# Block products for the down projection of three middle parts of the second feed-forward, added into x in DRAM

## The chip, the cores and the metric

The kernel runs on one core of a Trainium2 chip. The metric is the device time of one execution in microseconds (us); smaller is better. Three runs of the kernel before gave 1496.33, 1497.17 and 1498.62 us, so its median is 1497.17 us. One more execution was taken with the hardware profiler: it took 1496.28 us, of which the trace spans 1493.9 us, so 2.4 us lie around the span, and it is 0.9 us below the median.

The engines go by short names: PE is the matrix engine (TensorE), DVE is VectorE, ACT is ScalarE, POOL is GpSimd, SP is SyncE, which here only starts transfers. PSUM is the memory in eight banks that PE accumulates in, SBUF the large on-chip memory.

## The reference

One step through a two-layer backbone. Layer 0 has neighbourhood attention, layer 1 a gated linear recurrent unit, and behind each stands a gated feed-forward, with scale, shift and gate from a condition vector:

```
def _swiglu(x, w_gu, w_down):
    gate, up = jnp.split(x @ w_gu, 2, axis=-1)
    return (jax.nn.silu(gate) * up) @ w_down
...
        f_c = _swiglu(_modulate(ctx, norm_g[i, 1], sh2_c, sc2_c), ffn_w_gu[i], ffn_w_down[i])
        f_l = _swiglu(_modulate(lat, norm_g[i, 1], sh2_l, sc2_l), ffn_w_gu[i], ffn_w_down[i])
        ctx = ctx + g2_c[:, None, :] * f_c
        lat = lat + g2_l[:, None, :] * f_l
    y_prompt = _rms_norm(ctx, final_g)
    y_sample = _rms_norm(lat, final_g)
```

There are 128 context and 512 latent tokens, 640 in all; the model width is 1024 (8 tiles of 128) and the hidden width 2816 (22 tiles). The gate vector g2 differs between context and latent tokens. All is float32. The change bears on the down projection `@ w_down` of layer 1 and on the gated addition to the residual x behind it, and in a small way on the end of layer 0's attention.

## The kernel before, in words

**Numbers.** PE takes operands in a rounded 32-bit form (fp32r in the trace). Each operand is split in a high part (a cast) and a low part (the operand minus its high part), and each product is three matmuls: high by high, high by low, low by high. `split` does the two steps: the cast on ACT (L1496) and the subtraction on DVE (L1497). `chunk` (L251) is a plain product: for each of its k tiles of the inner dimension it issues the three matmuls of L252, L253 and L254, each 128 columns of weights by 320 tokens.

**The second feed-forward.** `ffn_halves` (L1220) walks over the 22 hidden tiles in six parts of 3, 3, 4, 4, 4 and 4 (CHN). For each hidden tile it makes gate and up, multiplies silu(gate) by up, splits the product in `hhi` and `hlo`, and when a part is done its rows of the down projection follow. Gate and up of one hidden tile are computed as one 2x2 block product with seven half products in place of eight (the scheme of Strassen and Winograd). Each of the seven is one call of `product` (L1167), three matmuls (L1171, L1172, L1173) for each of four k tiles. Its outputs accumulate in three PSUM banks: `mx` takes A11·B11, then S2·T2, then S3·T3, then A22·T4 on top of one another; `mm` takes A12·B21; `mc` takes S1·T1 and then S4·B22. A running sum that is needed by itself is copied out by ACT (`snap`, L1177) before PE may add the next product to the bank. In a part, `pair_a`, `pair_b` and `pair_c` hold these steps for a hidden tile; the weights' sums S1 to S4 are made by POOL (L1144), and cast and subtracted by ACT and DVE like the rest. `hidden` (L1187) ends a tile: multiply on DVE (L1190), cast on ACT, subtract on DVE, for each half of the tokens (320 each).

**The down projection of parts 1 to 5**, `project_part` (L603): for each of the eight output tiles and each half of the tokens, four k tiles (three in the first two parts) by three matmuls in a bank `mm`; `residual` (L569) then adds the gated sum to x in SBUF on DVE (L574), in pieces of 192, 128 and 320 columns, since the gate changes between context and latent tokens. A part of four tiles has 4·7·4·3 = 336 matmuls for gate and up, and 8·2·4·3 = 192 for the down projection. `project_last` does it for part 6, with the final norm.

**The order.** A scheduler simulates the program when it is built and sets the order of each engine's instructions; at the places in question the code adds a few rules of what issues after what (`issue_after`). On the chip every engine then runs its list in order, and a waiting instruction holds up all behind it. The plain down projection of a part can begin over the hidden tiles that are done, so at a part's end PE has a stock of matmuls that wait for nothing; the scheduler puts them between a bank's last matmul and the next one that has to wait for a copy of it.

**The end of the attention.** In layer 0 the output projection begins while the last heads are computed; the attention's result O is split tile by tile (ohi, olo), with rules for when the splits of the last tiles may issue (L1588).

## Time and profile before

| view | value |
|---|---|
| median of three runs | 1497.17 us |
| the profiled execution | 1496.28 us |
| its span | 1493.9 us |
| PE busy, share of the span | 1467.3 us, 98% |
| DVE busy | 1087.8 us, 73% |
| ACT busy | 730.4 us, 49% |
| POOL busy | 280.7 us, 19% |
| granted PE clock, mean | 0.997 of full speed |

Busy time of an engine is what its instructions took; matmuls are pipelined, so a matmul that lasts 0.31 us is followed by the next after 0.147 us. The views that matter here are the table by stretches of time (busy time of each engine within a stretch, with the number of instructions in brackets), the list of waits of one engine, the timeline (start, duration, engine, line, operation, tile written <- tiles read, and in square brackets the idle time before it with what ended it), the groups of instructions (count | busy us, mean ns of one | idle time before them) and the list of transfers (issuing queue, count, size, median time from issue to landing).

### The profile page before, as it was taken

Reading aid. Unit: us, or ns where it says so; the run is one execution under the profiler, and the core shown is the slowest. Engines: PE = TensorE matmul, PEld = TensorE weight load, DVE = VectorE, ACT = ScalarE, POOL = GpSimd, SP = SyncE. Lnnn points to the kernel's source line nnn. Section 1 sums busy time; section 2 is a strip of 40 time slices with the busy share of each in tenths; the row PEclk is TensorE's granted clock in tenths of the full one; section 3 lists DMA queues with packets and bytes.
Section 4 is the critical chain, followed back from the end, with each engine's and each line's share of the span. In section 5 each row is a group of like instructions: output and inputs, shape, how many; then the busy total and the mean of one; then the engine's idle time right before and its main releaser. Section 6 shows DMA issues by size and latency. Waiting matters only on the chain. (4 is left out here: it accounts for less than half of the span.)

```text
span 1493.9 us, 26401 instructions
## 1 busy us (share of the span) xinstructions
PE 1467.3 (98%) x10369; PEld 1438.2 (96%) x10369; DVE 1087.8 (73%) x2050; ACT 730.4 (49%) x1344; POOL 280.7 (19%) x357
## 2 busy tenths in 40 slices
PE   7999999999999999999999999999999999999997
PEld 4999999899999999999999999999999999999997
DVE  5788887868748779997766479985875566665655
ACT  5666766754334334422344298864634343424244
POOL 0212121100102222221210001112122332232311
PEclk9999999999999999999999999999999999999999
DMA  9554645445429999885863744266242131313111
GB/s 373 176 158 144 187 150 156 125 141 172 142 90 329 320 336 338 308 288 186 290 210 118 250 151 142 85 232 245 84 131 85 57 113 57 113 57 104 67 57 71
DMA packets 86427, 255.39 MB, mean 171 GB/s; under 512 B 9456, under 2 KB 22944, under 8 KB 86176
## 3 DMA queue, kind: packets, MB, share of 16 engines
q1 hardware_dynamic: 59408, 157.06, 32.1%
q0 software_dynamic: 26576, 96.49, 18.7%
q8 instruction: 81, 1.33, 0.3%
q14 instruction: 42, 0.34, 0.1%
q10 hardware_dynamic: 320, 0.16, 0.0%
HBM read 206.22 MB, written 43.53 MB: 167 GB/s over the span
## 5 line engine op out<-in xcount | busy, mean ns | idle before, releaser
L253 PE MATMUL mm<-big,whi 128*128 128x320 f32 (+3 forms) x1010 | 313.9, 311 | 1.9 <-DVE big L1497 1.9
L252 PE MATMUL mm<-big,whi 128*128 128x320 f32 (+3 forms) x1010 | 312.1, 311 | 3.2 <-ACT big L1496 2.1
L254 PE MATMUL mm<-big,wlo 128*128 128x320 f32 (+3 forms) x1010 | 313.7, 311 | 0.2 <-DVE wlo L1497 0.2
L291 DVE SCALAR_TENSOR_TENSOR mprod<-mraw,csb 128x1024 f32<-128x1024 f32 x160 | 195.9, 1224 | 19.2 <-DMA mraw<-in_wm 18.4
L252 PEld LDWEIGHTS mm<-big,whi 128*128 128x128 f32 x1010 | 190.1, 189 | 5.5 <-ACT big L1496 3.0
L253 PEld LDWEIGHTS mm<-big,whi 128*128 128x128 f32 x1010 | 190.9, 189 | 3.7 <-DVE big L1497 2.6
L254 PEld LDWEIGHTS mm<-big,wlo 128*128 128x128 f32 x1010 | 190.8, 189 | 1.5 <-DVE wlo L1497 0.4
L1496 ACT CAST whi<-raw 128x1024 fp32r<-128x1024 f32 (+2 forms) x103 | 105.7, 1026 | 152.0 <-PE mm L253 84.7
L1497 DVE TENSOR_TENSOR wlo<-raw,whi 128x1024 fp32r<-128x1024 f32 (+2 forms) x103 | 127.0, 1233 | 37.7 <-ACT whi L1496 37.3
L253 PE MATMUL mm<-big,whx 128*128 128x320 f32 (+3 forms) x443 | 137.4, 310 | 0.0
L254 PE MATMUL mm<-big,wlx 128*128 128x320 f32 (+3 forms) x443 | 137.1, 310 | 0.0
L252 PE MATMUL mm<-big,whx 128*128 128x320 f32 (+3 forms) x443 | 136.8, 310 | 0.0
L574 DVE SCALAR_TENSOR_TENSOR x<-mm,G,x 128x320 f32<-128x320 f32 (+3 forms) x202 | 81.5, 436 | 55.2 <-PE mm L254 50.1
L287 POOL DMA_DIRECT2D mraw<-in_wm x80 | 43.4, 543 | 313.5 <-DVE mprod L291 213.8
L254 PE MATMUL mx<-big,wlo 128*128 128x320 f32 (+3 forms) x318 | 99.2, 312 | 0.0
L253 PE MATMUL mx<-big,whi 128*128 128x320 f32 (+3 forms) x318 | 99.0, 311 | 0.0
L252 PE MATMUL mx<-big,whi 128*128 128x320 f32 (+3 forms) x318 | 98.7, 311 | 0.0
L253 PEld LDWEIGHTS mm<-big,whx 128*128 128x128 f32 x443 | 83.5, 189 | 0.0
L254 PEld LDWEIGHTS mm<-big,wlx 128*128 128x128 f32 x443 | 83.5, 189 | 0.0
L252 PEld LDWEIGHTS mm<-big,whx 128*128 128x128 f32 x443 | 83.4, 188 | 0.0
L253 PE MATMUL mx<-big,whx 128*128 128x320 f32 (+3 forms) x229 | 71.4, 312 | 0.0
L254 PE MATMUL mx<-big,wlx 128*128 128x320 f32 (+3 forms) x229 | 71.3, 312 | 0.0
(387 smaller groups left out, 3864.7 us busy)
## 6 DMA issues: line engine op xcount, KB each, us to landing
raw<-in_gu SPq DMA_DIRECT2D x84, 512.0 KB, 3.8
mraw<-in_wm POOLq DMA_DIRECT2D x80, 512.0 KB, 4.9
raw<-in_dn SPq DMA_DIRECT2D x24, 512.0 KB, 3.6
raw<-in_wqk SPq DMA_DIRECT2D x16, 512.0 KB, 4.0
sw<-in_wm SPq DMA_DIRECT2D x16, 512.0 KB, 10.2
mraw<-in_wi POOLq DMA_DIRECT2D x16, 512.0 KB, 6.4
kwi<-kwh POOLq DMA_DIRECT2D x16, 512.0 KB, 6.0
kwi<-kwl POOLq DMA_DIRECT2D x16, 512.0 KB, 5.6
```

The source lines that it names most:

```text
L252: nc.tensor.matmul(ps, hi[:, k], xhi[:, k, s], start=(k == 0), stop=False)
L253: nc.tensor.matmul(ps, hi[:, k], xlo[:, k, s], start=False, stop=False)
L254: nc.tensor.matmul(ps, lo[:, k], xhi[:, k, s], start=False, stop=(k == nk - 1))
L287: nc.gpsimd.dma_start(w, self.i["wm"][l * 6 + j - 2, f])
L291: nc.vector.scalar_tensor_tensor(prod, w, 1.0, self.csb[:, s], ALU.mult, ALU.mult, accum_out=out[:, s, f:f + 1])
L574: last = self.nc.vector.scalar_tensor_tensor(xs, ps[:, a - t0:b - t0], G[:, s, f:f + 1], xs, ALU.mult, ALU.add).ins
L1496: high = self.nc.scalar.copy(hi, v).ins
L1497: return high, self.nc.vector.tensor_tensor(lo, v, hi.bitcast(F32), ALU.subtract).ins
```

## The change

Parts 3, 4 and 5 (`BLOCKS = (2, 5)`) get another down projection. It is now a 2x2 block product as well: output tile f and output tile f+4 are the two block rows, the two halves of the tokens the block columns, and even and odd hidden tiles of the part the inner blocks. It takes seven half products of two k tiles, so 7·2·3 = 42 matmuls for a pair of output tiles and 4·42 = 168 for a part.

- `hidden` no longer writes the plain product h for these parts but what the scheme needs: of each pair of hidden tiles B11, T1 = B12 - B11, B21 and B22, and after the fourth also T2 = B22 - T1, T3 = B22 - B12 and T4 = B21 - T2. The last three go to a new tile `hx`.
- There is no room for `hx` beside x. So after part 2 x is stored to DRAM (`xd`, eight transfers of SP), `hx` takes its place in SBUF (the order names it x for that reason), and after part 5 x is loaded again by four transfers of SP.
- In `project_blocks` the weights of a pair of output tiles come by four transfers of 128 KB in place of one of 512 KB; POOL makes four sums of 128x256, ACT casts 768 and 1024 columns, where it cast 1024 for two output tiles, and DVE subtracts as many.
- The sums leave PSUM through `gated`, by ACT (scale by the gate) or by DVE (scale, and add an earlier copy); pieces that reach over the border between context and latent tokens take two instructions, of 192 and 128 columns. The results are added to `xd` in DRAM by accumulating transfers that POOL issues, three for a pair of output tiles.
- Apart from that, at the end of the attention the splits of O for k = 2 and 3 are to issue after the last Exp, and one after the other.

```
-    def project_part(self, w, hi, lo, gk):
+    def project_part(self, w, hi, lo, gk, store):
...
+                if store:
+                    self.nc.sync.dma_start(self.xd[(f + j) * P:(f + j) * P + P], self.x[:, f + j])
...
+        n = 2 * (j % 2) + c
+        if n == 0:
+            one = self.t([P, NTOK], F32, "ssq", 1, self.sb)
+            self.hb = [self.t([P, HT], F32, "sq", 2, self.sb) for _ in range(2)] + [one[:, 0:HT], one[:, HT:]]
+        t1, b12, b21, b22 = self.hb
+        h = self.hb[n]
+        nc.vector.tensor_tensor(h, u, g, ALU.mult)
+        if n == 1:
+            nc.vector.tensor_tensor(t1, b12, t1, ALU.subtract)
+            h = t1
+        self.split(hi, lo, h)
+        if n == 3:
+            for o, u, v in ((t1, b22, t1), (b12, b22, b12), (b21, b21, t1)):
+                nc.vector.tensor_tensor(o, u, v, ALU.subtract)
+            for m, v in enumerate((t1, b12, b21)):
+                self.split(self.hx[:, j // 2, m, 0], self.hx[:, j // 2, m, 1], v)
+
+    def gated(self, o, ps, G, f, t0, v=None):
+        for s, a, b in _pieces(t0, t0 + HT):
+            g, r = G[:, s, f:f + 1], slice(a - t0, b - t0)
+            if v is None:
+                self.nc.scalar.activation(o[:, r], ps[:, r], AF.Copy, scale=g)
+            else:
+                self.nc.vector.scalar_tensor_tensor(o[:, r], ps[:, r], g, v[:, r], ALU.mult, ALU.add)
+        return o
+
+    def project_blocks(self, w, gk, mid):
...
+        for f in range(KH):
+            raw = self.t([P, KT, P], F32, "raw", 3)
+            for a, (g, j) in enumerate(((f, 0), (f, 1), (f + KH, 1), (f + KH, 0))):
+                nc.sync.dma_start(raw[:, 2 * a:2 * a + 2], w[g].rearrange("p (k t) m -> p t k m", t=2)[:, j])
+            s = self.t([P, KT, P], F32, "sum", 2, self.sb)
...
+            for o, u, v, op in ((s1, a21, a22, ALU.add), (s2, s1, a11, ALU.subtract), (s3, a11, a21, ALU.subtract), (s4, a12, s2, ALU.subtract)):
+                nc.gpsimd.tensor_tensor(o, u, v, op)
...
+            def add(g, t0, o):
+                nc.gpsimd.dma_start(self.xd[g * P:g * P + P, t0:t0 + o.shape[1]], o, accum_op=ALU.add)
+
+            def kept(ps, g, t0):
+                return self.gated(self.t([P, HT], F32, "snap", 3, self.sb), ps, G, g, t0)
+
+            b = self.ps("mx")[:, 0:HT]
+            product(b, "A11", "B11", True)
+            m1 = kept(b, f, 0)
+            a = self.pg(False)[:, 0:HT]
+            product(a, "A12", "B21", True)
+            add(f, 0, self.gated(self.t([P, HT], F32, "sq", 2, self.sb), a, G, f, 0, m1))
+            c = self.ps("mc")[:, 0:HT]
+            product(c, "S1", "T1", True)
+            product(b, "S2", "T2", False)
+            u2 = kept(b, f, HT)
+            product(b, "S3", "T3", False)
+            u3 = kept(b, f + KH, HT)
+            o = self.t([P, NTOK], F32, "ssq", 1, self.sb)
+            self.gated(o[:, HT:], c, G, f + KH, HT, u3)
+            product(c, "S4", "B22", False)
+            add(f, HT, self.gated(self.t([P, HT], F32, "yo", 1, self.sb), c, G, f, HT, u2))
+            product(b, "A22", "T4", False)
+            self.gated(o[:, 0:HT], b, G, f + KH, 0)
+            add(f + KH, 0, o)
...
                     for k in range(4):
-                        with tc.issue_after(self.evac if k < 2 else self.low), tc.issue_after(self.cast) if k > 1 else nullcontext():
-                            self.split(ohi[:, k], olo[:, k], O[:, k])
+                        with tc.issue_after(self.evac) if k < 2 else tc.issue_after(self.low1), tc.issue_after(self.exp) if k > 1 else nullcontext(), tc.issue_after(self.cast) if k > 1 else nullcontext():
+                            high, low = self.split(ohi[:, k], olo[:, k], O[:, k])
```

The orders of the two programs show how matmuls and copies now stand. All tile numbers are those of the built programs; `mx_14360` is the same bank use in one row as in the next.

PE before, at the end of part 4, where the product S3·T3 of its last hidden tile (the 14th of 22) ends and A22·T4 adds to the same bank. The rows of L252, L253 and L254 are matmuls of the same part's down projection over its first hidden tiles.

```order
L1173 MATMUL mx_14360<-big_11765,wlx_14404 128x320
L253 MATMUL mm_14583<-big_11765,whi_14579 128x320
L254 MATMUL mm_14583<-big_11764,wlo_14580 128x320
L254 MATMUL mm_14597<-big_11764,wlo_14580 128x320
L252 MATMUL mm_14597<-big_11764,whi_14579 128x320
L253 MATMUL mm_14597<-big_11765,whi_14579 128x320
...
L1171 MATMUL mx_14360<-xt_11353,wuh_14440 128x320
```

PE after the change, the same step of the same hidden tile.

```order
L1174 MATMUL mx_14484<-big_11765,whx_14527 128x320
L1175 MATMUL mx_14484<-big_11765,whx_14527 128x320
L1176 MATMUL mx_14484<-big_11765,wlx_14528 128x320
L1174 MATMUL mx_14484<-xt_11353,wuh_14568 128x320
L1175 MATMUL mx_14484<-xt_11353,wuh_14568 128x320
L1176 MATMUL mx_14484<-xt_11353,wul_14569 128x320
```

Before, nine matmuls of the down projection stood between the end of one product in the bank and the start of the next; after the change the next product stands directly behind.

ACT after the change, at the end of the same part and the first pair of output tiles (the casts to `x_13265` write T2, T3 and T4 to `hx`; L1218 is `gated`).

```order
L1596 CAST big_11764<-ssq_14543 128x320
L1596 CAST x_13265<-sq_14544 128x320
L1596 CAST x_13265<-sq_14545 128x320
L1596 CAST x_13265<-ssq_14543 128x320
L1218 ACTIVATE snap_14744<-mx_14712,G_1498_8333 128x192
L1218 ACTIVATE snap_14744<-mx_14712,G_1498_8333 128x128
L1218 ACTIVATE snap_14753<-mx_14712,G_1498_8333 128x192
L1218 ACTIVATE snap_14753<-mx_14712,G_1498_8333 128x128
```

The three casts for `hx` and four pieces that empty the bank `mx_14712` have come in; on PE the products S2·T2, S3·T3 and A22·T4 of that pair of output tiles stand directly behind one another in this bank.

DVE at the end of a part, after the change (`g` is silu(gate) or its sum, `ssq` and `sq` hold B and T parts, L1210 is `hidden`'s subtractions).

```order
L1185 TENSOR_TENSOR g_14691<-mm_14678,snap_14676 128x320
L1597 TENSOR_TENSOR wlx_14875<-sum_14865,whx_14874 128x1024
L1203 TENSOR_TENSOR ssq_14543<-c_2351_14613,g_14642 128x320
L1210 TENSOR_TENSOR sq_14544<-ssq_14543,sq_14544 128x320
L1210 TENSOR_TENSOR sq_14545<-ssq_14543,sq_14545 128x320
L1597 TENSOR_TENSOR big_11765<-ssq_14543,big_11764 128x320
L1210 TENSOR_TENSOR ssq_14543<-ssq_14543,sq_14544 128x320
L1597 TENSOR_TENSOR x_13265<-sq_14544,x_13265 128x320
L1597 TENSOR_TENSOR x_13265<-sq_14545,x_13265 128x320
L1220 SCALAR_TENSOR_TENSOR sq_14728<-mm_14721,G_1498_8333,snap_14719 128x320
L1597 TENSOR_TENSOR x_13265<-ssq_14543,x_13265 128x320
```

Before, the same place had the multiply of L1190, one subtraction of L1497 and then the additions to x of L574; now three subtractions of L1210 and three of L1597 stand behind the last multiply, ahead of what the next products read. Over the whole program PE's list goes from 9492 to 9420 rows, DVE's from 1817 to 1859 and ACT's from 1203 to 1306.

More of the change, by code (lines that the diff above doesn't have):

```diff
@@ L49 @@
 CHN = (3, 3, 4, 4, 4, 4)
+BLOCKS = (2, 5)
 START = (
@@ L145, in __init__ @@
         self.n, self.ng, self.nu, self.hold, self.late = 0, 0, 0, None, []
-        self.anchor, self.pbufs, self.lastq, self.whole, self.nraw, self.px = None, {}, {}, False, 2, None
+        self.anchor, self.pbufs, self.lastq, self.whole, self.nraw, self.px, self.low = None, {}, {}, False, 2, None, None
     def nm(self, s):
@@ L1189, in hidden @@
         hi, lo = [t[:, j, c * HT:c * HT + HT] for t in (self.hhi, self.hlo)]
-        nc.vector.tensor_tensor(g, u, g, ALU.mult)
-        self.split(hi, lo, g)
+        if self.hx is None:
+            nc.vector.tensor_tensor(g, u, g, ALU.mult)
+            self.split(hi, lo, g)
+            return
+        n = 2 * (j % 2) + c
+        if n == 0:
+            one = self.t([P, NTOK], F32, "ssq", 1, self.sb)
+            self.hb = [self.t([P, HT], F32, "sq", 2, self.sb) for _ in range(2)] + [one[:, 0:HT], one[:, HT:]]
@@ L1223, in ffn_halves @@
         f0 = 0
+        self.hx = None
         for ci, n in enumerate(CHN):
```

48 lines of the change are left out of this document (42 added, 6 removed).

## Prediction

> **What bounds the kernel now.** I read the page's first two parts, then the table by stretches of time for the second feed-forward, then PE's own list of waits there. The page says who is busy:
>
> ```profile
> PE 1467.3 (98%) x10369; PEld 1438.2 (96%) x10369; DVE 1087.8 (73%) x2050; ACT 730.4 (49%) x1344; POOL 280.7 (19%) x357
> PE   7999999999999999999999999999999999999997
> PEclk9999999999999999999999999999999999999999
> ```
>
> PE has work in every slice at full granted clock. The three middle parts are three equal stretches (columns: stretch, its length, then busy us and count of PE, weight loads, DVE, ACT, POOL, and last the clock, the DMA share and GB/s):
>
> ```profile
> 1160.60:1238.10 77.50, 76.83 (x521) 76.20 (x520) 50.19 (x79) 32.64 (x52) 23.02 (x17) 1.00 0.27 82
> 1238.10:1315.60 77.50, 77.50 (x529) 77.38 (x529) 46.22 (x73) 30.20 (x48) 22.07 (x16) 1.00 0.27 82
> 1315.60:1393.20 77.60, 77.60 (x531) 77.48 (x530) 46.77 (x73) 30.14 (x48) 21.92 (x16) 1.00 0.27 82
> ```
>
> A part is 336 + 192 = 528 matmuls, and 77.5 / 528 = 0.147 us each: PE is the bound without a gap. All that it waits for from 1100 to 1440 us are two entries (total, times, longest):
>
> ```profile
> PE mm L252 <- DVE x L574: 1.0, 2, 0.5
> PE mx L1171 <- ACT snap L1177: 0.2, 1, 0.2
> ```
>
> So a matmul less is worth 0.147 us, a wait on PE costs what it lasts, and the other engines have room: DVE 46 of 77 us, ACT 30, POOL 22. The question is whether the change, which takes matmuls out, puts waits in.
>
> **Step 1, matmuls.** Each block part has 168 matmuls for 192. 3·24 = 72 go, and the order confirms it: PE's list has 72 rows less. 72 × 0.147 = **-10.6 us**.
>
> **Step 2, copies out of a bank.** PE may not add to a bank until ACT has copied it. What that costs when no other matmul stands between can be read where the feed-forward opens:
>
> ```profile
> 1083.55 0.30 PE L1173 MATMUL mx<-big,wlx 128*128 128x320 f32 x1
> 1083.89 0.43 ACT L1177 COPY snap<-mx 128x320 f32<-128x320 f32 x1 [2.33 <-PE mx L1173]
> 1084.37 0.41 PE L1171 MATMUL mx<-big,whx 128*128 128x320 f32 x1 [0.52 <-ACT snap L1177]
> 1084.62 0.31 PE L1172 MATMUL mx<-big,whx 128*128 128x320 f32 x1
> 1084.77 0.31 PE L1173 MATMUL mx<-big,wlx 128*128 128x320 f32 x1
> ```
>
> From the last matmul's start to the copy's are 0.34 us, the copy lasts 0.43, and PE goes on 0.05 later. 1084.37 - 1083.55 = 0.82 in place of 0.147; the first matmul after an idle stretch also holds up its follower by 0.25 in place of 0.147. The loss is 0.82 - 0.15 + 0.10 = 0.77 us, although the idle entry reads 0.52. That the waits above are so few is the work of the plain down projection's matmuls. In one of the parts the copies stood behind a cast of 1.05 us on ACT, and the matmuls of L252 to L254 hid nearly all:
>
> ```profile
> 1220.11 1.05 ACT L1496 CAST whi<-raw 128x1024 fp32r<-128x1024 f32 x1 [1.00 <-DMA raw<-in_dn]
> ...
> 1221.07 0.75 ACT L1177 COPY snap<-mx 128x320 f32<-128x320 f32 x2
> 1221.07 0.31 PE L254 MATMUL mm<-big,wlo 128*128 128x320 f32 x1
> ...
> 1221.54 0.42 PE L1171 MATMUL mx<-xt,wuh 128*128 128x320 f32 x1 [0.16 <-ACT snap L1177]
> ```
>
> This cover shrinks. In the order after the change the step from S3·T3 to A22·T4 of a part's last hidden tile has lost its nine matmuls (in the three block parts alike), and in `project_blocks` the products S2·T2, S3·T3 and A22·T4 of the first pair of output tiles and of the last stand directly behind one another, with two copies between them; only the two pairs in the middle have each other's matmuls to fill in. That is per part one copy in one piece and four in two pieces of 192 and 128 columns, as u2 and u3 hold the tokens over the border. No scaled copy from PSUM in these pieces is in the trace; the nearest rows, by mean ns:
>
> ```profile
> L557 ACT ACTIVATE big<-x,A 128x192 fp32r<-128x192 f32 x16 | 7.2, 453 | 11.5 <-DVE x L574 11.5
> L557 ACT ACTIVATE big<-x,A 128x128 fp32r<-128x128 f32 x16 | 6.2, 390 | 0.0
> L694 ACT ACTIVATE r<-mm 128x128 f32<-128x128 f32 x16 | 3.6, 282 | 4.0 <-DVE r L692 3.9
> L705 ACT COPY K<-mm 128x192 f32<-128x192 f32 x7 | 2.2, 312 | 0.0
> ```
>
> Back to back instructions of ACT overlap by about 0.1 (two copies of 0.43 took 0.75 above), so two pieces take 0.31 + 0.28 - 0.1 = 0.5 by the lower rows, and 0.45 + 0.39 - 0.1 = 0.74 by the scaled rows. I take 0.66, nearer to the scaled rows, as the new copies carry a scale too: loss 0.34 + 0.66 + 0.05 - 0.15 + 0.10 = 1.0 us. Per part 0.8 + 4 × 1.0 = 4.8, **+14.4 us** in all. The low end is 15 × 0.77 = 11.6, the high end one in three copies behind a cast of 1.05 us, +5, so 19.
>
> **Step 3, the combinations at a part's end.** The last hidden tile now ends in T2, T3 and T4, and S2·T2 of the first pair of output tiles needs T2's low part. In the order 28 matmuls of other products stand between the last one of S4·B22 and that, 29 × 0.147 = 4.26 us. Against it runs a chain on DVE (mean ns of one):
>
> ```profile
> L1497 DVE TENSOR_TENSOR wlx<-sum,whx 128x1024 fp32r<-128x1024 f32 x35 | 43.9, 1253 | 22.0 <-ACT whx L1496 22.0
> L1497 DVE TENSOR_TENSOR big<-g,big 128x320 fp32r<-128x320 f32 x34 | 23.3, 684 | 10.3 <-ACT big L1496 10.3
> L1182 DVE TENSOR_TENSOR g<-mc,snap 128x320 f32<-128x320 f32 x17 | 8.3, 489 | 11.0 <-PE mc L1173 11.0
> L1190 DVE TENSOR_TENSOR g<-mx,g 128x320 f32<-128x320 f32 x17 | 8.3, 488 | 27.4 <-PE mx L1173 27.4
> ```
>
> An operation of 0.49 gives way to the next after about 0.41. The chain is 0.34 to its start, two sums of 0.41, the weights' subtraction 1.17 (SiLU on ACT fits beside it), multiply, T2 and T3 at 0.41, B22's low part 0.5, T4 0.41 and T2's low part 0.6: 0.34 + 0.82 + 1.17 + 1.23 + 0.5 + 0.41 + 0.6 = 5.1. PE waits 0.85 a part, **+2.6 us**; bounds 0 (the weights' subtraction issues sooner) and 6 (every low part at 684, DVE late by one more operation of 1.25). What waits behind this on PE is everything.
>
> **Step 4, the accumulating transfers.** No transfer in the trace accumulates. The nearest go to the same tensor, plain:
>
> ```profile
> xd<-x SPq DMA_DIRECT2D x8, 320.0 KB, 2.2
> xd<-x POOLq DMA_DIRECT2D x16, 160.0 KB, 6.4
> ```
>
> and an issue costs POOL itself 0.54:
>
> ```profile
> L287 POOL DMA_DIRECT2D mraw<-in_wm x80 | 43.4, 543 | 313.5 <-DVE mprod L291 213.8
> ```
>
> The buffers that they read (`ssq`, `yo`) have one slot each, so the next pair's evacuation on DVE waits for the landing, and S4·B22, which needs the bank `mc`, for the evacuation. A pair's product takes 42 × 0.147 = 6.2 us, a landing with its issue about 7; in the order only the third pair has few matmuls (six) ahead of S4·B22. I take 0.5 a part, **+1.5 us**, bounds 0 (earlier evacuation) and 2.1 a part (7 + 0.5 for the copy out + 0.8 for the two additions on DVE, against 6.2). On SP the reload of x waits for the last addition and stands ahead of the last hidden tile's weights; by the order those are due some 15 us later, against 10.4 for the slowest reload of this kind, so it costs nothing unless landings double.
>
> ```profile
> x<-xd SPq DMA_DIRECT2D x4, 640.0 KB, 10.4
> ```
>
> In the Trainium skill, "DMA: Bandwidth & Descriptors", section "Anatomy of one DMA — SWDGE (gpsimd) path", a POOL transfer is fitted as 2.0 us plus its bytes over 436 KB per us, which for 160 KB is an estimate of 2.4 us. The row says 6.4, and the row decides; by the page this term would be 0.
>
> **Step 5, load.** Per part DVE gains 14 operations for T1 to T4 at 0.49 to 0.68 (+7.5), subtracts 4 × 768 columns more (estimated at three quarters of 1.25, +4) and has less to evacuate (-2): 55 us. ACT gains six casts (0.46 each by my estimate, as a copy of 320 columns takes 0.43), 4 × 768 columns of casts at three quarters of 1.05, and the copies at about 2.2 a pair: +15, 45 us. POOL gains sixteen sums of half the size (22.07 / 16 / 2 = 0.7 each) and twelve issues at 0.54: +18, 40 us. None reaches 77, so none becomes the bound by its load; what it costs in order is in steps 2 and 3.
>
> **Step 6, the attention's end.** Here PE waits for the split of O:
>
> ```profile
> 287.48 2.61 ACT L1496 CAST big<-big 128x640 fp32r<-128x640 f32 x4
> ...
> 290.95 0.57 ACT L777 COPY PT<-tp 128x512 f32<-128x512 f32 x1
> 291.65 0.41 PE L253 MATMUL mm<-big,whi 128*128 128x320 f32 x1 [1.93 <-DVE big L1497]
> ```
>
> After the change two of the four casts issue later and four transposes move into the gap. The split that PE waits for still comes at about the same time, since DVE's part hangs on its own queue, so the gap isn't filled but partly used: **-0.8 us**, bounds -2.3 (gap gone) and +1 (the casts late).
>
> **Sum.** -10.6 + 14.4 + 2.6 + 1.5 - 0.8 = +7.1. From the profiled 1496.3 (span 1493.9 and 2.4 around it) that gives 1503.4; the median of the runs lies 0.9 higher, so **1504.3 us**.
>
> **The rivals.** *B, waits at their low end*: copies 0.77 each, step 3 hidden, landings in time: -10.6 + 11.6 - 0.8 = +0.2, 1497.4. For it: ACT is idle half the time. Against it: the two-piece copies are two instructions. *C, the other side, faster*: the order of the built program leaves fewer direct waits than I read, or PE loses 0.25 a copy, as with some matmuls in between: 15 × 0.25 = 3.8, -10.6 + 3.8 - 0.8 = -7.6, 1489.6. It decides below (10.6 + 0.8 - 3) / 15 = 0.56 us a copy. Against it stands the 0.77 of the direct row. *D, POOL's sums hold up DVE in the chain of step 3.* Sixteen sums of 128x256 more run in each of these parts. The trace shows what a sum does to DVE:
>
> ```profile
> 1081.27 0.48 DVE L1007 TENSOR_TENSOR big<-x,big 128x320 fp32r<-128x320 f32 x1
> 1081.43 1.47 POOL L1144 TENSOR_TENSOR sum<-raw,raw 128x512 f32<-128x512 f32 x1 [24.68 <-DVE wlx L1497]
> 1081.67 1.58 DVE L1007 TENSOR_TENSOR big<-c,big 128x320 fp32r<-128x320 f32 x1
> ```
>
> The same operation takes 0.48 alone and 1.58 beside a sum, 1.1 more. Two such meetings in each chain give 3 × 2.2 = 6.6: 1510.9. In the Trainium skill, "SBUF — State Buffer", section "Who interferes with whom", an operation of DVE with two SBUF inputs and one of POOL that reads SBUF exclude each other, the later one waiting for the whole of the earlier; all nine such operations in the chain are of that kind. The two rows agree (1.58 against 0.48). By the rule the chain could meet a sum more often than my means hold. *E, slow landings*: an accumulating transfer reads and writes, and at 12.8, twice 6.4, the third pair's S4·B22 waits 6.4 longer in each part: +19, 1523.5.
>
> **How the numbers follow.** The forecast 0.56, B 0.17, C 0.10, D 0.10, E 0.07. A measurement can tell 0.2% of this time, 3 us, from no change, so B is the same (0.17), C faster (0.10), the others slower (0.73). The range leaves out E and most of C: low 1494 for B with the attention's gap gone (1497.4 - 1.5, and a little of C), high 1513 for D with step 4 at its bound.
>
> **What the changed profile would show.** Step 1: PE's row count 72 lower. Step 2: waits of PE on ACT's `gated` copies, about 0.5 to 0.9 each, 12 in two pieces and 3 in one. Step 3: in each part one wait of PE on DVE for T2's low part near 0.9. Step 4: landings of the additions to `xd` near 6.4. A part of 77.5 us would be near 80. Wrong would be: a part shorter than 75, which makes step 2 too dear; or many DVE operations near 1.5 us (D); or landings over 10 (E). Step 6 shows in the gap at 291.65.

## The result, and the profile after

The changed kernel takes 1544.38 us, median of four runs (1542.97 to 1545.79), against 1496.75 for the kernel before: 1.0312 times as long, 95% interval 1.0299 to 1.0325. The forecast was 1504.3, at most 1513. The direction was right and the size was not: 47.6 us more, where 7.1 were expected.

The profiled execution took 1545.79 us. Its page, first parts:

```profile
span 1544.0 us, 26723 instructions
PE 1484.4 (96%) x10297; PEld 1443.4 (93%) x10297; DVE 1134.4 (73%) x2092; ACT 770.5 (50%) x1446; POOL 360.2 (23%) x441
PE   7999999999999999999999999999999889897997
PEclk9999999999999999999999999999999989999999
```

PE has 72 matmuls less and is nevertheless busy for 17 us more: a busy PE is not a PE at its peak. The hint stands in the lowest row, where the granted clock has a dip (the 8) that this row of the kernel before did not have. The table by stretches, with the ends of parts 3, 4 and 5 and the block products behind them in the long rows:

```profile
1180.00:1220.00 40.00, 39.68 (x270) 39.41 (x269) 30.92 (x45) 18.58 (x33) 15.33 (x13) 1.00 0.26 79
1220.00:1280.00 60.00, 49.88 (x289) 47.62 (x288) 29.77 (x49) 25.59 (x50) 29.40 (x30) 0.89 0.55 105
1280.00:1310.00 30.00, 29.71 (x199) 28.93 (x198) 25.11 (x32) 15.34 (x28) 14.69 (x12) 1.00 0.32 89
1310.00:1370.00 60.00, 50.21 (x293) 46.68 (x292) 35.47 (x53) 27.47 (x54) 32.01 (x32) 0.91 0.52 103
```

In a long stretch PE stands still for 10 of 60 us and runs at a mean clock of 0.9 besides; between them, while hidden tiles are made, it stands still for 0.3 to 0.6 us and keeps its clock. PE's list of waits from 1100 to 1490 us (total, times, longest):

```profile
PE mx L1250 <- ACT snap L1218: 9.4, 12, 0.8
PE mx L1174 <- ACT snap L1180: 7.2, 3, 4.3
PE mx L1251 <- DVE x L1597: 5.3, 3, 1.8
PE mx L1250 <- ACT x L1596: 3.7, 3, 1.7
PE mx L1174 <- ACT whi L1596: 2.8, 1, 2.8
PE mx L1250 <- DVE sq L1203: 1.8, 2, 1.0
PE mx L1251 <- DVE big L1597: 1.6, 3, 0.6
```

From the top: the copies between block products; the copy ahead of A22 of each part's last hidden tile; the low part and the high part of T2; the weights of the last hidden tile in part 6; and B11 of the last hidden tile but one, for A11·B11.

**Where the time went.** One program point stands in both traces: the first matmul of A22 of the feed-forward's first block-wise hidden tile, at 1087.01 before and 1090.29 after; the last group of matmuls starts at 1486.23 and 1536.28. So 399.2 us became 446.0, 46.8 more. Matmul by matmul, the time from one start to the next beyond 0.147 us (for 320 columns) adds up, from 1100 to 1480 us, to 40.7 us behind named waits (before: 1.6) and 19.8 where nothing is waited for (before: 0.9). With the 72 matmuls: -10.6 + 39.1 + 18.9 = 47.4. Of the 18.9 us about 15 are PE at half clock: the trace's clock record has 37.5 us at half between 1100 and 1480 us, none there before, and the matmuls in those stretches that wait for nothing lose 15.1. The other 4 are mostly matmuls right behind a gap, each of which holds its follower for 0.25 us in place of 0.147. Here is the last pair of output tiles of part 3, on the timeline:

```profile
1268.74 0.41 PE L1250 MATMUL mx<-x,whx 128*128 128x320 f32 x1 [0.77 <-ACT snap L1218]
...
1270.66 0.41 PE L1250 MATMUL mx<-x,whi 128*128 128x320 f32 x1 [0.77 <-ACT snap L1218]
1270.91 0.31 PE L1251 MATMUL mx<-x,whi 128*128 128x320 f32 x1
1271.06 0.31 PE L1252 MATMUL mx<-x,wlo 128*128 128x320 f32 x1
1271.20 0.41 PE L1250 MATMUL mx<-x,whi 128*128 128x320 f32 x1
1271.41 0.47 PE L1251 MATMUL mx<-x,whi 128*128 128x320 f32 x1
1271.68 0.47 PE L1252 MATMUL mx<-x,wlo 128*128 128x320 f32 x1
```

and the clock there (the last three numbers of a row are the clock, the DMA share and GB/s):

```profile
1268.00:1270.00 2.00, 1.15 (x6) 0.89 (x6) 0.00 (x0) 0.76 (x3) 0.00 (x0) 1.00 0.58 120
...
1272.00:1274.00 2.00, 2.00 (x9) 2.00 (x9) 0.00 (x0) 0.53 (x1) 0.00 (x0) 0.50 0.00 0
...
1276.00:1280.00 4.00, 4.00 (x29) 4.00 (x29) 2.76 (x5) 2.39 (x4) 2.40 (x3) 1.00 0.79 113
```

Two gaps of 0.77 us, 1.9 us apart, and half a microsecond after the second the clock is 0.50: matmuls follow each other after 0.267 us, until about 1274.6. Nothing is waited for in that stretch, PE counts as fully busy, and it does nine matmuls where it would do fourteen. The Trainium skill, "TensorE: Matmul & The Clock Gate", section "Part 1: The HAM clock gate (the "warmup" mystery)", has this gate: a window of about 3.4 us in which PE is idle halves its clock, and one that is busy restores it. The 3.4 us of half clock agree; the short form of its rule, no gap longer than about 3.4 us, does not: here 1.5 us of idleness in two pieces were enough.

### The profile page after: what moved, and what is told of

Read it like the earlier page. It is cut to its first block, busy times and chain, and to the rows that moved or that the text cites. A ratio compares the mean times of both kernels' runs of the same rounds, so it can differ in the third digit from the quotient of the medians.

```text
span 1544.0 us, 26723 instructions
## 1 busy us (share of the span) xinstructions
PE 1484.4 (96%) x10297; PEld 1443.4 (93%) x10297; DVE 1134.4 (73%) x2092; ACT 770.5 (50%) x1446; POOL 360.2 (23%) x441
## 5 line engine op out<-in xcount | busy, mean ns | idle before, releaser
L254 PE MATMUL mm<-big,whi 128*128 128x320 f32 (+2 forms) x818 | 254.1, 311 | 1.2 <-DVE big L1597 1.2
L253 PE MATMUL mm<-big,whi 128*128 128x320 f32 (+2 forms) x818 | 253.1, 311 | 2.0 <-ACT big L1596 1.6
L255 PE MATMUL mm<-big,wlo 128*128 128x320 f32 (+2 forms) x818 | 254.2, 311 | 0.0
L292 DVE SCALAR_TENSOR_TENSOR mprod<-mraw,csb 128x1024 f32<-128x1024 f32 x160 | 195.7, 1223 | 19.8 <-DMA mraw<-in_wm 19.1
L1597 DVE TENSOR_TENSOR wlo<-raw,whi 128x1024 fp32r<-128x1024 f32 (+2 forms) x103 | 123.7, 1201 | 61.6 <-ACT whi L1596 61.2
L253 PEld LDWEIGHTS mm<-big,whi 128*128 128x128 f32 x818 | 153.9, 189 | 3.7 <-ACT big L1596 1.9
L254 PEld LDWEIGHTS mm<-big,whi 128*128 128x128 f32 x818 | 154.6, 189 | 2.5 <-DVE big L1597 1.5
L255 PEld LDWEIGHTS mm<-big,wlo 128*128 128x128 f32 x818 | 154.4, 189 | 1.1
L254 PE MATMUL mm<-big,whx 128*128 128x320 f32 (+3 forms) x439 | 136.0, 310 | 0.0
L253 PE MATMUL mm<-big,whx 128*128 128x320 f32 (+3 forms) x439 | 135.6, 309 | 0.0
L253 PE MATMUL mx<-big,whi 128*128 128x320 f32 (+3 forms) x318 | 98.8, 311 | 0.0
L254 PE MATMUL mx<-big,whi 128*128 128x320 f32 (+3 forms) x318 | 98.8, 311 | 0.0
L254 PEld LDWEIGHTS mm<-big,whx 128*128 128x128 f32 x439 | 82.8, 189 | 0.0
L253 PEld LDWEIGHTS mm<-big,whx 128*128 128x128 f32 x439 | 82.6, 188 | 0.0
L1597 DVE TENSOR_TENSOR wlx<-sum,whx 128x1024 fp32r<-128x1024 f32 x52 | 67.4, 1297 | 16.4 <-ACT whx L1596 15.9
L253 PE MATMUL mx<-big,whx 128*128 128x320 f32 (+3 forms) x233 | 72.5, 311 | 0.0
L254 PE MATMUL mx<-big,whx 128*128 128x320 f32 (+3 forms) x233 | 72.4, 311 | 0.0
```

Of the source, the lines that this page charges most:

```text
L253: nc.tensor.matmul(ps, hi[:, k], xhi[:, k, s], start=(k == 0), stop=False)
L254: nc.tensor.matmul(ps, hi[:, k], xlo[:, k, s], start=False, stop=False)
L255: nc.tensor.matmul(ps, lo[:, k], xhi[:, k, s], start=False, stop=(k == nk - 1))
L292: nc.vector.scalar_tensor_tensor(prod, w, 1.0, self.csb[:, s], ALU.mult, ALU.mult, accum_out=out[:, s, f:f + 1])
L1597: return high, self.nc.vector.tensor_tensor(lo, v, hi.bitcast(F32), ALU.subtract).ins
```

## The experiments

All ratios are to the kernel before, run beside each on the same chip. "Stretch" is the time between the two program points above in the profiled execution (399.2 before, 446.0 for the change). Differences from the change that the text gives in us are of medians. The kernel before, run beside them, had medians from 1496.32 to 1500.12 us on the different chips, so between runs of different chips two or three us are open.

| run | median, us | ratio, 95% interval | stretch, us |
|---|---|---|---|
| att_only | 1496.1 | 0.9994, 0.9983 to 1.0005 | 398.7 |
| one_part | 1513.59 | 1.0112, 1.0092 to 1.0132 | 414.9 |
| fill_copies | 1537.32 | 1.0271, 1.0251 to 1.0291 | 442.4 |
| act_order | 1538.26 | 1.0273, 1.0251 to 1.0296 | 442.9 |
| late_reload | 1541.03 | 1.0277, 1.0259 to 1.0295 | 440.7 |
| quiet_pool | 1537.55 | 1.0271, 1.0250 to 1.0292 | 440.4 |
| sums_dve | 1535.96 | 1.0266, 1.0244 to 1.0288 | 438.2 |
| interleaved | 1523.49 | 1.0181, 1.0165 to 1.0196 | 428.5 |
| interleaved_quiet | 1535.46 | 1.0265, 1.0238 to 1.0291 | 437.6 |
| inter_dve_late | 1510.29 | 1.0076, 1.0055 to 1.0097 | 411.5 |
| early | 1505.73 | 1.0062, 1.0037 to 1.0087 | 411.0 |
| early_dve | 1501.75 | 1.0019, 1.0006 to 1.0033 | 404.0 |
| early_swap | 1513.77 | 1.0108, 1.0091 to 1.0125 | 418.5 |
| early_swap_pool | 1518.35 | 1.0140, 1.0121 to 1.0160 | 421.8 |
| swap_act | 1521.63 | 1.0147, 1.0129 to 1.0166 | 423.6 |
| swap_act2 | 1516.39 | 1.0121, 1.0098 to 1.0145 | 418.1 |
| tail_order | 1505.35 | 1.0051, 1.0036 to 1.0067 | 406.9 |
| tail_order_pool | 1518.18 | 1.0131, 1.0109 to 1.0153 | 419.3 |

**Which part of the change.** `BLOCKS` decides which parts use block products: (9, 9) is none, (4, 5) is part 5 alone.

```
-BLOCKS = (2, 5)
+BLOCKS = (9, 9)
```

> No part of the feed-forward uses block products; only the new order of the casts at the attention's end is left. In the profile of the change the attention's end lies 1.2 us better against the profile before than what stood ahead of it. If that is its whole effect: 1495.5 us, 1.3 below the kernel before. If part of the loss came from there: above 1499.

0.9 us less, and the interval holds both no change and the 1.3 expected. The loss is not there.

```
-BLOCKS = (2, 5)
+BLOCKS = (4, 5)
```

> Only part 5 uses block products (x is stored after part 4 and loaded after part 5). Theory that each block part loses by itself, through its own waits and the half clock behind them: part 5 lost about a third, so 1496.75 - 1.3 + 16 = 1511, between 1507 and 1517. Rival, that the loss comes from the store and reload of x and the late weights of the last hidden tile, which are there once however many parts are changed: above 1525.

1.0112 is +16.8 us, about a third of the loss, and the store and reload of x, which happen once, are in it. So most of the loss comes part by part.

**The half clock.** Extra matmuls are put behind the products ahead of a copy, and the next product behind them.

```
+            ends = f in (0, KH - 1)
...
+            w2 = warm(p2, 5) if ends else p2
+            with self.tc.issue_after(w2):
+                p3 = product(b, "S3", "T3", False)
```

> The change with extra matmuls into an unused bank, whose results nobody reads: five behind S2·T2 and five behind S3·T3 of the first and the last pair of output tiles, six behind S3·T3 of a part's last hidden tile, 78 in all (11.5 us of work on PE at 0.147 us). PE's waits for the copies end when they did, but PE is busy in them. Theory that idle gaps of 0.8 us close behind one another halve PE's clock: the drop behind the last pair of each part goes (about 1.8 us each), and the ones at the first pair get shorter, 3 x 4 in all: 1532 to 1538. Rival, that the half clock has another cause (load, transfers): 1544 or up to 10 us above.

7.1 us less than the change, with 78 matmuls more. The waits for T2 stay (4.1 and 5.3 us in all); the gaps at the copies are only filled. At the last pair of part 3, where five matmuls now stand in each gap:

```profile
1268.00:1270.00 2.00, 1.96 (x13) 1.61 (x11) 0.08 (x1) 0.76 (x3) 0.00 (x0) 1.00 0.71 254
1270.00:1272.00 2.00, 1.96 (x14) 1.80 (x13) 0.60 (x2) 0.99 (x3) 0.00 (x0) 1.00 0.02 8
1272.00:1274.00 2.00, 2.00 (x16) 2.00 (x15) 0.00 (x0) 0.49 (x2) 0.57 (x1) 1.00 0.00 0
```

The clock stays at 1.00, here and at the last pairs of parts 4 and 5. But this alone doesn't show that filling did it there: in the run late_reload (below), which changes nothing at these places, both gaps are open and the clock stays at 1.00 as well, at all three last pairs. Two rows of its timeline and two of its table by stretches, at the last pair of part 3:

```profile
1268.70 0.41 PE L1250 MATMUL mx<-x,whx 128*128 128x320 f32 x1 [0.77 <-ACT snap L1218]
...
1270.62 0.41 PE L1250 MATMUL mx<-x,whi 128*128 128x320 f32 x1 [0.77 <-ACT snap L1218]
...
1268.16:1271.57 3.41, 2.10 (x12) 1.83 (x13) 0.68 (x2) 1.49 (x5) 0.00 (x0) 1.00 0.46 154
1271.57:1274.98 3.41, 3.41 (x25) 3.41 (x24) 0.52 (x2) 1.57 (x3) 0.87 (x1) 1.00 0.00 0
```

The clock records of the traces point to the reason. From 1100 to 1480 us the clock changes only on a fixed raster of 3.41 us, whose phase differs from execution to execution. In the change's trace both gaps lie in one step of the raster, and the next step runs at half clock:

```profile
1267.84:1271.26 3.42, 1.88 (x11) 1.49 (x11) 0.68 (x2) 1.68 (x5) 0.02 (x1) 1.00 0.55 156
1271.26:1274.67 3.41, 3.41 (x15) 3.41 (x14) 0.00 (x0) 0.53 (x1) 0.44 (x1) 0.50 0.00 0
```

PE is idle for 1.54 us of the first step there, in late_reload for 1.31, since a border of the raster at 1268.16 cuts the first gap. In fill_copies a border falls between the two places, so its clock there can't be told from one without filling. What it does show is at the first pairs, where the half clock lasts one step in each part in place of two; from 1100 to 1480 us it falls from 37.5 us to 17.1. In all twenty traces every drop in that time follows a step in which PE is idle for 1.45 us or more. Load and transfers as such don't halve the clock: at the last pairs late_reload does the same work as the change, without a drop.

**The copy ahead of A22.** In the timeline of the change, the end of part 3:

```profile
1222.45 0.83 ACT L1596 CAST whi<-raw 128x768 fp32r<-128x768 f32 x1 [3.04 <-DMA raw<-in_dn]
1222.55 0.31 PE L1176 MATMUL mx<-big,wlx 128*128 128x320 f32 x1
...
1223.31 1.14 DVE L1597 TENSOR_TENSOR wlo<-raw,whi 128x768 fp32r<-128x768 f32 x1 [3.11 <-ACT whi L1596]
...
1225.41 0.46 ACT L1596 CAST big<-sq 128x320 fp32r<-128x320 f32 x1 [2.13 <-DVE sq L1205]
1225.78 1.04 ACT L1596 CAST whx<-sum 128x1024 fp32r<-128x1024 f32 x1
...
1226.72 0.74 ACT L1180 COPY snap<-mx 128x320 f32<-128x320 f32 x2
...
1227.19 0.63 PE L1174 MATMUL mx<-xt,wuh 128*128 128x320 f32 x1 [4.34 <-ACT snap L1180]
```

The last matmul of S3·T3 starts at 1222.55, and its copy runs four microseconds later, since ACT takes its list in order: first a cast that waited 3.04 us for block weights, then one that waited 2.13 for DVE, then one of the weights' sums. DVE was late for the same reason: its subtraction `wlo`, which waited 3.11 us for that first cast, stands ahead of the `sq` that the second cast waits for. The copy itself was ready by about 1222.9. act_order puts the block weights' casts behind it.

```
+                with self.tc.issue_after(self.kept3):
+                    self.split(hi[:, 0:n], lo[:, 0:n], src[:, 0:n])
```

> The change, with ACT's casts of the block weights put behind the last hidden tile's copy of the third product. Theory that PE's waits of 4.3, 0.9 and 1.9 us there come from those casts, which wait for weights and sums while a ready copy stands behind them: they fall to 0.8 each, 4.8 us less, and with the half clock behind them 5 to 8 less: 1536 to 1540. Rival, that the copies are late for another reason, or that the casts are now late for the first pair of output tiles: 1543 or more.

The three waits fall from 7.2 to 1.7 us, as expected, and 6.1 us are won, but the casts are now late for T2: the waits for its high part grow from 3.7 to 12.9. Part of the gain is a wait moved.

**POOL's sums.** First, later sums put behind the first addition to x:

```
+                with self.tc.issue_after(self.pw) if f > 1 else nullcontext():
+                    nc.gpsimd.tensor_tensor(o, u, v, op)
```

> The change, with POOL's sums for the third and fourth pair of output tiles and for the next hidden tile put behind the first addition to x, so that POOL makes no sums while DVE forms T2, T3 and T4. Theory that these sums double DVE's operations in that chain (1.57 and 1.71 us where 0.49 and 0.7 are usual): PE's waits for T2, 3.1 us and more in each part, fall to 1 to 1.5, and the half clock behind them gets shorter: 6 to 10 us less, 1534 to 1538. Rival, that the chain is long by its own instructions and ACT's queue: within 3 of 1544; and if the sums are then late for the third pair, above 1547.

6.8 us less. The waits for T2 (9.0 us) are gone from PE's list; in their place stand 4.9 for the bank that DVE empties into `ssq`, 4.0 for `whi` in three waits behind the first pairs of output tiles and one of 1.8, 2.2 for `wlx`, and a wait of 4.0 in part 6 where there were 2.8; the 6.0 in front of A22 are hardly less than before. Both theories are right in part: the sums do delay the chain, and they are late when they go second. What they do to DVE in the change, on the timelines of DVE and POOL at the end of part 4 (`big` is a low part, L1185 the first sum behind S4, L1210 makes T2 and T3; each takes about 0.49 where POOL makes no sum, `wul` 0.7):

```profile
1321.95 1.71 DVE L1597 TENSOR_TENSOR wul<-raw,wuh 128x512 fp32r<-128x512 f32 x1 [0.69 <-ACT wuh L1596]
1323.19 1.61 POOL L1147 TENSOR_TENSOR sum<-sum,raw 128x512 f32<-128x512 f32 x1
1323.58 1.57 DVE L1597 TENSOR_TENSOR big<-ssq,big 128x320 fp32r<-128x320 f32 x1
1325.08 0.48 DVE L1185 TENSOR_TENSOR g<-mc,snap 128x320 f32<-128x320 f32 x1
...
1327.17 1.45 POOL L1147 TENSOR_TENSOR sum<-raw,raw 128x512 f32<-128x512 f32 x1 [2.36 <-DVE wlx L1597]
1327.53 2.92 DVE L1210 TENSOR_TENSOR sq<-ssq,sq 128x320 f32<-128x320 f32 x2
1328.58 1.52 POOL L1147 TENSOR_TENSOR sum<-raw,sum 128x512 f32<-128x512 f32 x1
```

and the same two operations in quiet_pool, where POOL makes no sums beside them:

```profile
1322.63 0.89 DVE L1210 TENSOR_TENSOR sq<-ssq,sq 128x320 f32<-128x320 f32 x2
```

The sum at 1325.08 could have started 2.1 us earlier, 0.34 after the start of S4's last matmul at 1322.62. It has one input in PSUM and takes 0.48 like elsewhere. In the Trainium skill, "SBUF — State Buffer", section "Who interferes with whom", operations of DVE with two SBUF inputs and of POOL that read SBUF shut each other out for the whole of the earlier one; these rows agree.

Next, the block weights' sums on DVE:

```
-                nc.gpsimd.tensor_tensor(o, u, v, op)
+                nc.vector.tensor_tensor(o, u, v, op)
```

> The change, with the sixteen sums of the block weights in each part made by DVE in place of POOL. DVE gets 48 operations of 0.4 to 0.5 us more and POOL 48 less of about 1. If the lock between POOL and DVE and POOL's slow sums are what delays the chain: 1530 to 1538. If DVE's queue is what delays it: 1548 or more.

8.4 us less, although DVE has 48 operations more. The wait ahead of A22 falls from 7.2 to 0.4: weights come earlier (at the end of part 3 SP has issued the twelve transfers of the first three pairs by 1215.6 us, in the change by 1220.6), since POOL's sums no longer hold their slots. The waits for T2 stay (5.3 and 3.5): there it is the sums for the next hidden tile, still on POOL, that meet DVE.

**The reload.** It is put behind the last hidden tile's weights on SP.

```
+                    with self.tc.issue_after(self.lastraw):
+                        self.load_x(self.xd)
```

> The change, with the four transfers that load x again put behind the last hidden tile's weights on SP. Theory that the reload, which waits 11 us on SP for the last addition and for PE's last use of the old slot, holds up those weights and so makes PE's wait of 2.8 us in part 6 with half clock behind it: that wait goes, 3 to 5 us less, 1539 to 1541. Rival, that those weights are late for another reason (their slot): within 2 of 1544.

3.3 us less by the medians (1.0277 against 1.0312, and 5.3 us by the stretch), and the wait of 2.8 for `whi` is gone from the list.

**Products that cover each other.** Two pairs of output tiles alternate, in a fixed order.

```
+            with self.in_order(ORDERED[:1]):
...
+                both = [steps(f + i, W[i], one[:, i * HT:i * HT + HT]) for i in range(2)]
+                for _ in range(7):
+                    for g in both:
+                        next(g)
```

> The change, with two pairs of output tiles at a time, their products alternating in a fixed order (A11, A11, A12, A12, S1, S1, S2, S2, S3, S3, A22, A22, S4, S4) in two banks each, so that six matmuls of the other pair (0.88 us) stand in each wait for a copy; results go to x by four additions of 160 KB in place of three. Theory: the twelve waits of 0.8 us for copies fall to about 0.1 and the half clock behind the last pair goes (1.8 us a part): 9.4 + 5 us, 1528 to 1532. The waits for T2 and in front of A22 of the last hidden tile stay. Rival, that the waits only move to DVE's additions: 1538 or more.

20.9 us less, more than expected. The twelve waits of 0.8 us are gone from PE's list altogether; its largest entries are now those at a part's end:

```profile
PE mx L1174 <- ACT snap L1180: 9.7, 6, 3.6
PE mx L1257 <- DVE x L1613: 5.4, 3, 1.8
```

> Both of the two before: alternating products, and POOL's later sums put behind the first addition. If their gains add: 1519 to 1526. If the copies' waits had been all: the same as the alternating products alone.

A miss: 12 us above the alternating products alone. Once two pairs run together, the third and fourth pair's weights are due earlier, and sums that are held back are late (casts and subtractions of `whx`, `wlx` and `whi` cost PE 7.4 and 3.5 us).

> Alternating products, sums on DVE and the late reload, without the fixed order at a part's end. If the three gains add (21, 8 and 4 below the change): 1508 to 1514. If the sums on DVE bring nothing once the copies are covered: 1518 to 1522.

34.1 us less than the change: 21, 8 and 3 make 32, so they add within what medians of different chips can tell. The half clock from 1100 to 1480 us is down from 37.5 us to 3.4.

**A part's end.** In `early`, products of the block part stand between those of the last hidden tile, and the next part's first hidden tile in front of what needs T2.

```
+            self.pair_b(tail, n - 1)
+            x, y = pair(0)
+            next(x)
+            next(y)
+            self.pair_c(tail, lambda: next(y))
+            start()
+            order = [x, y, x] + [x, y] * 4
+            for g in order:
+                next(g)
```

> Alternating products in pairs as before, and a fixed order at a part's end: A11 of the first two pairs of output tiles stands between S3 and A22 of the last hidden tile, one S1 behind A22, and the next part's first hidden tile (24 matmuls) between S4 and what needs T2; x is loaded again behind the last hidden tile's weights. Theory that every large wait of the change lies where PE has nothing else in its order: the waits in front of A22 and for T2 and the half clock behind them go, 1500 to 1510. If ACT's and DVE's queues are late by more than the 3.5 us that this covers: 1512 to 1522.

> The same with the block weights' sums on DVE in place of POOL. Sums on DVE took PE's wait in front of A22 away where nothing covered it, so if POOL's slow sums still hold up the weights: 3 to 8 us below the version with the sums on POOL, 1495 to 1507. If DVE's queue is now the bound at a part's end: above it.

1505.73 and 1501.75: both as the first theory had it, and sums on DVE are worth 4.0. Of the 34 us in PE's list of waits for the change, about 10 are left in early_dve, at these places:

```profile
PE mx L1174 <- ACT snap L1180: 5.3, 3, 3.4
PE mc L1174 <- DVE g L1185: 3.4, 3, 1.8
PE mx L1256 <- ACT snap L1218: 1.6, 3, 0.5
```

Six more runs asked whether these are late weights or load, and whether the block products can pay.

> The version with the fixed order and the sums on DVE, with the order at a part's end changed once more: S4 of the hidden tile before the last goes ahead of the last one's S2, S1 and S3, and its A22 stands between S3 and A22 of the last; the first products of the block weights come behind A22, where they are due 3.5 us later. Theory that the 5.3 us in front of A22 and the 3.4 us in front of S4 that are left come from block weights that are late: both fall to below 1.5 in all, 1492 to 1497, at or below the kernel before. If ACT's queue keeps the copy behind the weights' casts wherever they stand: 1500 to 1504 as before.

> The same with the block weights' sums on POOL, as the change has them. If sums on POOL cost by holding weights and DVE up at a part's end: 3 to 6 us above the same with sums on DVE. If that went with the weights' due time: within 2.

The two waits went as expected, and a new one of 12.8 us came in front of S4 of the tile before, so 12 us were lost. Sums on POOL cost 4.6 more.

> The version with the swapped order and sums on DVE, with ACT's casts of all block weights put behind the last hidden tile's copy of the third product, so that no cast that waits for late weights stands ahead of a copy or of a sum. Theory that the 12.8 us in front of S4 of the hidden tile before the last come from such a cast (it waited 2.6 us for its weights ahead of the copies) and not from load: they fall below 3, and with the half clock 13 to 16 us go, 1497 to 1502; what is late then shows as waits of A11 for the casts. Rival, that ACT and DVE have too much to do there: above 1508.

> The same, with S2 of the last hidden tile ahead of S4 of the one before, so that twelve more matmuls (1.76 us) stand in front of what waited. If a remainder of that wait is left in the run beside it, it goes: up to 3 us below it, 1495 to 1500. If nothing is left there: within 1.5 of it.

Both missed, and lie above early_swap. With the casts behind the copies the wait in front of S4 fell to 8.2 in the first and 2.0 in the second; but in both, 8.1 and 5.4 us of waits for the cast and the low part of A22's weights stood beside it, where early_swap had 1.7 and 2.7. These weights have one slot, and the swapped order put the A22 of two hidden tiles next to each other; why the waits grew with the later casts was not tried.

> Alternating products, sums on DVE, late reload, ACT's casts of all block weights behind the last hidden tile's copy of the third product, and at a part's end this order: the last hidden tile's products as they were, then the next part's first hidden tile (24 matmuls), then A11, A12 and S1 of two pairs of output tiles (36 matmuls), then what needs T2. Nothing covers the copy in front of A22 (0.8 us a part), but nothing late stands ahead of it, and the block weights are due 7 us later than in the version with A11 in front of A22. Theory that late casts at the head of ACT's queue are what was left there: waits of 3 to 5 us in all, little half clock, 1489 to 1494, below the kernel before. If load is the cause: 1499 or more.

> The same with the block weights' sums on POOL, as the change has them. If POOL's sums still cost by delay and by the lock with DVE: 3 to 6 us above the version with sums on DVE. If the later due time hides them: within 2.

tail_order missed its 1489 to 1494 too. It is the one version with block products in which the clock never drops between 1100 and 1480 us, and late weights cost it only one wait of 0.5 us. But 11.5 us of short waits are left in three groups, the larger two between a hidden tile's own products, which the kernel before hides with the plain down projection:

```profile
PE mx L1174 <- ACT snap L1180: 5.0, 6, 1.6
PE mc L1174 <- DVE g L1185: 4.3, 6, 0.9
PE mx L1257 <- ACT c L1218: 2.2, 3, 0.8
```

Here sums on POOL cost 12.8 us more. So late weights were a part of it, and what is left is short waits behind ACT and DVE with nothing to cover them. No version with block products is faster than the kernel before: the best, early_dve, is 0.2% slower.

## Why the prediction was right or wrong

**Right in direction, and in a part of the mechanism.** Step 1: 72 matmuls went. The forecast's thesis was that the change gives PE's cover away and that waits cost more than 10.6 us; that is what happened. What failed are four terms: the copies ahead of A22 in step 2 (0.8 us each, where PE waited 7.2 in all), the chain of step 3 (0.85 a part, measured 2.5 to 3.5), the reload in step 4 (put at nothing, worth at least 3.3), and the rate of 0.147 us for every matmul that remains, which has no term for the half clock (about 15). PE's waits for B11 of the last hidden tile but one (1.8 and 1.6) had no term either.

**Step 2, the copies: right for twelve, wrong for three.** The twelve copies in two pieces make idle entries of 0.77 to 0.83 us; their pieces take 0.42 and 0.36, near the 0.66 in all that was taken. The three in one piece, ahead of A22, were put at 0.8 each and left 4.3, 0.9 and 1.9. A copy was priced by its own length, as if ACT had nothing ahead of it; the bound (one copy in three behind a cast of 1.05) did not consider that the cast itself waits. act_order and sums_dve showed both halves of this: the cast at the head of the queue, and the sums that make its weights late.

**Step 3, the combinations at a part's end: mis-sized.** 0.85 a part was expected; T2's two waits are 2.5 to 3.5. The chain's operations were right and two of their times wrong. In all three parts T2 and T3 take 2.9 us in place of 0.8, beside POOL's sums. And the chain was to begin 0.34 us after S4's last matmul: in part 3 it does, but in part 5 DVE comes to the first sum 1.2 us after it, and in part 4 2.5 us, behind two operations of 1.71 and 1.57 us that run beside POOL's sums. This is rival D, which was given a chance of its own when it belonged to the forecast: the two rows of the profile before that carried it (0.48 and 1.58) spoke for it, and the lock between DVE and POOL that it names shows in quiet_pool, where the waits go with the sums. D counts all nine operations of the chain as having two inputs in SBUF; two of them, the sums behind S4, read one from PSUM, and stay at 0.48.

**Step 4: the additions right, the reload wrong.** The accumulating transfers land after 3.4 to 4.4 us (median), faster than the plain row of 6.4, and PE's waits for them are 0.4 in all; rival E was far off. The reload of x, counted as free for 15 us of slack, held up the last hidden tile's weights: 3.3 us by the medians of late_reload.

**Step 6** cannot be told from nothing: by the ratio 0.9 less, interval -2.5 to +0.7.

**The step that is missing: the half clock.** No term and no rival held that gaps which lie close together slow PE behind them. That is about 15 of the 46.8 us. The page of before could not show it there, as it had no such gaps; but a rate was assumed (0.147 us for every matmul that remains) that holds only for a PE without gaps. fill_copies showed it in part: with PE busy in the gaps, 17.1 us at half clock are left of 37.5. How much of it one execution has seems to hang on the phase of the raster as well. With the waits (39.1 where 18.5 were summed) this makes the miss: of the 39 us between the stretch's 46.8 and the 7.9 that steps 1 to 4 gave it, about 15 are half clock, 4 are mostly followers of gaps, and 20.6 are waits that were sized too small (together 0.6 more than the stretch).

## What to carry to other kernels

An engine that is the bound has its waits hidden by whatever independent work stands in its order; a change that removes work from it removes cover first, so count the places that lose cover, and price each by what stands ahead of the releasing instruction in its queue, including what that one waits for. On PE, add the half clock: two gaps of less than a microsecond within two microseconds can cost about as much again behind them, and filling gaps with useless matmuls can pay (here 7.1 us). The fast algorithm with dependent accumulations did not pay here in any version; it came nearest where two pairs alternated and other work stood at a part's end.

## What the runs showed of the hardware that was not expected

Two gaps of 0.77 us within 1.9 us halved the clock for 3.41 us at all three last pairs of the change's trace, and at none of the three in late_reload's. A gap of 0.78 and one of 0.62, 1.7 apart, did not in the change's trace at 1311 us, where a border of the raster at 1312.2 parts them; in late_reload's a gap of 0.82 and one of 0.62 did, in one step from 1309.13 to 1312.54. The parts are 27 steps of the raster apart (92.2 us), so the three places of one trace have one phase and count as one trial. Single gaps of up to 1.6 us did not halve the clock in tail_order. Nor does the idle time of a step alone decide: over the runs from 1100 to 1480 us, steps with 1.45 us of idleness were followed by half clock, and others with up to 1.89 were not. Once halved, the clock stayed so for another step where PE was idle for 0.62 us or more in the step, and went back to full where it was idle for 0.59 or less.

The same program point, ahead of all that was changed in the feed-forward, was reached between 1084.2 and 1091.5 us in the twenty profiled executions. In the change's, 4 us are lost in the first 25 us, where PE stays at half clock for longer than before. So differences of a few microseconds between two single traces are better read from a stretch than from the span.
